# Starting the value projection on unscaled x, and taking the norms' roots on columns of tokens

## The chip, the cores and the metric

The kernel runs on one core of a Trainium2 chip. The metric is the device time of one execution in microseconds. Five engines take part, each with its own in-order queue: TensorE (matmuls, shown as PE, its weight loads as PEld), VectorE (DVE), ScalarE (ACT), GpSimd (POOL) and SyncE (SP), which issues all the transfers.

## What is computed

```python
# x: (1, 2048, 1024) f32; two layers, then one more RMSNorm
h = rms_norm(x, w0)                        # x * rsqrt(mean(x*x) + 1e-6) * w0
u, v, g = split(h @ w_in, 3)               # each 2048 wide
v = layer_norm(gelu(v))                    # over its 2048 columns
s = einsum('gts,bnsgc->bntgc', tril(w_s), v in chunks of 128 tokens) + b_s
x = x + (gelu(u) * s * silu(g)) @ w_out
h = rms_norm(x, w1)
xb, g = split(h @ w_in_b, 2)               # each 1536 wide
xc = causal conv of width 4 over xb        # then two gates of 12 heads of 128
y = linear recurrence over the tokens      # a*h + sqrt(1-a^2)*(i*xc)
x = x + (y * silu(g)) @ w_out_b
return rms_norm(x, wf)
```

## The kernel before

Activations are held transposed, features on the 128 partitions and tokens on the free axis. The 2048 tokens go in two blocks (`i`, NB = 2) of 1024, each in two halves (`th`) of 512. Every f32 factor is split in two rounded parts (`split`, L78: a cast on ScalarE, L80, a difference on VectorE, L81), and a product is three matmuls (`mm3`, L284 to 288).

A block runs through these stages. `a_values` (L570) makes v: for each of four column groups `c` of 512, for each of eight feature tiles `kt`, it multiplies token tiles of 128 (stationary) with the weights (moving, 512 columns), 12 matmuls for a half's four token tiles and one `kt`. The sums stand in PSUM, `pj` (three buffers of two banks) and `pb` (two of one bank). `evict` applies Gelu, takes statistics and stores v to memory. Group 0 goes by halves, the other three take both halves together. Then come `a_gates` (u and g with a Strassen scheme over 2x2 blocks, the spatial gate, `ps`), four `out_round`s, `b_branch` (layer 1: `px`, `pg`, and per head the gates `pr`, `pi`), `b_out` (`po`) and the final norm with `store`.

Weights come from a single ordered list, `stream`. `take(key)` (L270) issues the loads up to 8 entries ahead of the key and the splits up to 4 ahead. In block 0 six of the eight items of layer 0's output weights are prepared and stored away for both blocks (`keep`) during groups 1 to 3, two in each, and the last two in the gate stage.

The norm: `Norm.add` squares on ScalarE and adds on VectorE into `acc` (128 x 512). `finish` (L398) sums over the partitions with one matmul against ones, so the sum of a token stands in all partitions, and calls `rsqrt` (L372) on 128 x 512: Identity and Sqrt on ScalarE, then a reciprocal and three more operations on VectorE for one Newton step. It is used 12 times: for the two halves of each block at layer 0, at layer 1 (`finish_b`) and at the end (`end_f`).

At the start, `first` (half 0 of block 0) is loaded, normed, scaled and split before `a_values` is called; `step(0, 0)` does the same for `second`. `step` also makes Strassen's sums (`Sums`) and sets up the spatial mask and bias (`setup_sgu`) and the recurrence's constants (`setup_lru`). At layer 1, `hb` is x times the norm's weight without 1/rms, and 1/rms is multiplied in when `px` and `pg` are read (`xb` L718, `sg` L739).

The order of the instructions on each engine is fixed when the program is built: a scheduler takes the traced instructions by priority as its estimate of times says that they are ready and have a buffer.

Of the kernel before, what the change touches and what calls it, by code (L numbers as in the profile page):

```python
# [14 lines left out]
P = 128  # L15
D = 1024
# [30 lines left out]

AG = ((0, 0), (1, 0), (0, 1), (1, 1))


@with_exitstack
def trunk(ctx: ExitStack, tc: tile.TileContext, xT, WI, WV, WB, WO, WG, par, wsT, bs, outT):
# [14 lines left out]
    def pb(name):  # L67
        return pbp.tile([P, T], F32, tag="pb", name=name)

    def wk(name):  # L70
        return work.tile([P, 1032], F32, tag="wk", name=name)[:, :TB].rearrange(
            "p (a t) -> p a t", a=2
        )

# [12 lines left out]
    def wop(name):  # L87
        return wops.tile([P, 2, T], F32R, tag="wop", name=name)

    def prep_v(i, c):  # L90
        st = {}

        def load(k):
            def f():
                st[k] = raws.tile([P, 2, T], F32, tag="raw", name=f"rv{i}_{c}_{k}")
                nc.sync.dma_start(
                    st[k], WV[c * 8 + 2 * k : c * 8 + 2 * k + 2].rearrange("k p t -> p k t")
                )
            return f

        def make(kt):
            def f():
                t = wop(f"wv{i}_{c}_{kt}")
                split(t, st[kt // 2][:, kt % 2, :])
                return t
            return f

        return [((i, "v", c, kt), make(kt), load(kt // 2) if kt % 2 == 0 else None)
                for kt in range(8)]

    def prep_item(i, m, keep=False, use=True):

# [150 lines left out]
    def advance(c, n, f):  # L263
        while c[0] < len(stream) and c[1] <= n:
# [2 lines left out]
            c[0] += 1  # L267
            c[1] += key is not None

    def take(key):  # L270
        def load(key, make, load):
            if load is not None:
                load()

        def make(key, make, load):
            t = make()
            if key is not None:
                ready[key] = t

        advance(loads, at[key] + FAR, load)  # L280
        advance(makes, at[key] + LOOK, make)
        return ready.pop(key)

    def mm3(out, sh, sl, mh, ml, first, last):  # L284
# [10 lines left out]
    def col(c):  # L295
        return pp[:, c : c + 1]

    ones = const.tile([P, P], F32, name="ones")
    eps = const.tile([P, 2], F32, name="eps")
    halo = const.tile([P, NH, 3], F32, name="halo")  # L300
    state = const.tile([P, NH], F32, name="state")
    c8 = const.tile([P, NH], F32, name="c8")
# [78 lines left out]
    class Norm:  # L381
# [5 lines left out]
        def add(self, t, eng=nc.vector):  # L387
            for kk in range(2):
# [178 lines left out]
        nc.sync.dma_start(yd[a].rearrange("h p k t -> p h k t")[:, :, j % 2, :], t)  # L567


    def a_values(i, bt, step):  # L570
# [4 lines left out]
        def mm(c, kt, w, tt, out):  # L575
            n, a = kt // 2, kt % 2
            b = bt[a, tt // 4][n // 2]
            ts = slice((tt % 4) * P, (tt % 4 + 1) * P)
            mm3(
                out, b[:, 0, n % 2, ts], b[:, 1, n % 2, ts], w[:, 0], w[:, 1], kt == 0, kt == 7  # L580
            )

        def evict(c, tt, srcs):
            t = wk(f"v{i}_{c}_{tt}")
            if len(srcs) == 1:
                nc.scalar.activation(t, srcs[0], AF.Gelu_apprx_tanh)
            else:
                for k in range(2):
                    nc.scalar.activation(t[:, k], srcs[k], AF.Gelu_apprx_tanh)
# [4 lines left out]
        w = [take((i, "v", 0, kt)) for kt in range(8)]  # L594
        for th in range(2):
            acc = [pj(f"pv{i}_0_{th}{k}") for k in range(2)]
            for kt in range(8):
                for tt in range(4):
                    mm(0, kt, w[kt], 4 * th + tt, acc[tt // 2][:, tt % 2])
                step(0, 8 * th + kt)  # L600
            for k in range(2):
                evict(0, 4 * th + 2 * k, [acc[k]])
        for c in range(1, 4):
            acc = [pj(f"pv{i}_{c}_{k}") for k in range(3)]
            last = [pb(f"pv{i}_{c}_{k}") for k in range(3, 5)]
            for kt in range(8):
                wt = take((i, "v", c, kt))
                for tt in range(8):
                    out = acc[tt // 2][:, tt % 2] if tt < 6 else last[tt - 6]
                    mm(c, kt, wt, tt, out)  # L610
                step(c, kt)
            for k in range(3):
                evict(c, 2 * k, [acc[k]])
            evict(c, 6, last)
# [89 lines left out]
    class Head:  # L704
# [9 lines left out]
        def conv(self, px, rb):  # L714

            n = self.n
            xb = work.tile([P, 1032], F32, tag="wk", name=f"xb{self.id}")
# [207 lines left out]
    bt = {}  # L925
    first.split(bt)
    second = Half(0, 1)
    pending = []
    for i in range(NB):
        tpa = {}  # L930

        def step(c, kt):
            if c > 0:
                return
            if kt == 0:
                if i == 0:
                    second.load(True)
                    second.norm()
                    second.scale()
                second.split(bt)  # L940
            if kt in (1, 3) and pending:
                pending.pop(0)()
            if kt in (8, 12):
                g = (kt - 8) // 4
                have = {1: bt[0, 0][g], 2: bt[1, 0][g], 3: bt[1, 1][g]}
                hx = first.x | second.x
                q = {(a, th): hx[a, th, g] for a in range(2) for th in range(2)}
                tpa[g] = Sums(f"ha{i}_{g}", q, have)
                tpa[g].make(*((5, 6, 7, 4) if g == 0 else (5,)))
            if kt == 14:  # L950
                if i == 0:
                    setup_sgu()
                    setup_lru()
                else:
                    load_sgu(i)

        values = a_values(i, bt, step)
        tpa[1].make(6, 7, 4)
        yd = a_gates(i, [tpa[0].o, tpa[1].o], values)

# [174 lines left out]
```

## Time and profile before

| | us |
|---|---|
| median of 3 runs (2287.63 to 2290.79) | 2289.09 |
| the profiled execution | 2292.71 |
| its span, first to last instruction | 2291.0 |
| TensorE busy | 2213.1 (97%) |
| VectorE busy | 1575.7 (69%) |
| ScalarE busy | 1057.3 (46%) |

Busy time is the union of an engine's instructions; a waiting engine is not busy. The idle time in front of an instruction is what its engine did nothing in, and the name behind it tells what ended that. The columns PEclk give TensorE's granted clock, where 1.00 is 2.4 GHz and 0.50 is 1.2 GHz. On the profile's chain of waits TensorE has 85%, VectorE 8%, transfers 3%.

### The profile page before, as it was taken

Reading aid. Unit: us, or ns where it says so; the run is one execution under the profiler, and the core shown is the slowest. Engines: PE = TensorE matmul, PEld = TensorE weight load, DVE = VectorE, ACT = ScalarE, POOL = GpSimd, SP = SyncE. Lnnn points to the kernel's source line nnn. Section 1 sums busy time; section 2 is a strip of 40 time slices with the busy share of each in tenths; the row PEclk is TensorE's granted clock in tenths of the full one; section 3 lists DMA queues with packets and bytes.
Section 4 is the critical chain, followed back from the end, with each engine's and each line's share of the span. In section 5 each row is a group of like instructions: output and inputs, shape, how many; then the busy total and the mean of one; then the engine's idle time right before and its main releaser. Section 6 shows DMA issues by size and latency. Waiting matters only on the chain.

```text
span 2291.0 us, 25466 instructions
## 1 busy us (share of the span) xinstructions
PE 2213.1 (97%) x9872; PEld 1821.4 (80%) x9872; DVE 1575.7 (69%) x1936; ACT 1057.3 (46%) x1377; POOL 63.2 (3%) x82
## 2 busy tenths in 40 slices
PE   5999999999999899999999999999999989999996
PEld 4787888888788688888788888888878868888884
DVE  6957787676777677775693266676669766776736
ACT  4434444443215677774342144444412347767611
POOL 0000000000000001000000000000000000110000
PEclk9999999999999999999999999999999989999998
DMA  4788353327764122226143233322487512321411
GB/s 148 262 310 307 127 180 111 110 83 270 276 231 141 51 88 88 95 102 231 37 166 110 74 110 111 102 94 100 162 311 256 194 60 69 106 92 65 176 45 74
DMA packets 124040, 327.84 MB, mean 143 GB/s; under 512 B 9616, under 2 KB 26128, under 8 KB 123920
## 3 DMA queue, kind: packets, MB, share of 16 engines
q1 hardware_dynamic: 123920, 326.22, 41.0%
q8 instruction: 77, 1.26, 0.2%
q14 instruction: 43, 0.35, 0.0%
HBM read 232.34 MB, written 93.85 MB: 142 GB/s over the span
## 4 chain that ended last, share of the span: by engine, by line
PE 85%; DVE 8%; DMA 3%; issue 2%; ACT 1%; SPq 0%; DVEq 0%; ACTq 0%
PE J L286 20%; PE pv L286 13%; PE pg L286 11%; PE px L286 10%; PE po L286 10%; PE X L286 6%; PE Y L286 5%; PE Z L286 3%; PE ps L653 2%; PE pr L286 2%; PE pi L286 2%; DMA keep<-wc 1%; DVE ya L81 1%; DMA x<-in_xT 1%; DVE xr L873 0%
## 5 line engine op out<-in xcount | busy, mean ns | idle before, releaser
L286 PE MATMUL pv<-wv,b 128*128 128x512 f32 x1536 | 357.9, 395 | 19.6 <-ACT b L80 15.8
L286 PE MATMUL J<-ha,w 128*128 128x512 f32 x1536 | 368.9, 391 | 0.5 <-DVE u_2b L494 0.5
L286 PEld LDWEIGHTS pv<-wv,b 128*128 128x128 f32 x1536 | 291.4, 190 | 86.4 <-ACT b L80 17.8
L286 PEld LDWEIGHTS J<-ha,w 128*128 128x128 f32 x1536 | 287.6, 188 | 61.5 <-DVE u_2b L494 0.9
L286 PE MATMUL po<-yb,wo 128*128 128x512 f32 x1152 | 265.6, 392 | 2.6 <-DVE xr L862 2.6
L286 PE MATMUL pg<-hb,wb 128*128 128x512 f32 x1152 | 266.6, 390 | 0.0
L286 PE MATMUL px<-hb,wb 128*128 128x512 f32 x1152 | 266.6, 390 | 0.0
L286 PEld LDWEIGHTS po<-yb,wo 128*128 128x128 f32 x1152 | 217.3, 189 | 49.7 <-DVE xr L862 3.0
L286 PEld LDWEIGHTS pg<-hb,wb 128*128 128x128 f32 x1152 | 217.1, 188 | 46.0
L286 PEld LDWEIGHTS px<-hb,wb 128*128 128x128 f32 x1152 | 216.3, 188 | 45.8 <-PE st_b L400 0.5
L286 PE MATMUL J<-b,w 128*128 128x512 f32 x768 | 186.8, 391 | 0.3 <-DVE w L81 0.3
L286 PE MATMUL X<-ya,w 128*128 128x512 f32 x768 | 184.1, 390 | 2.3 <-ACT ya L80 1.3
L286 PEld LDWEIGHTS X<-ya,w 128*128 128x128 f32 x768 | 143.6, 188 | 34.0 <-DVE x L550 2.2
L286 PEld LDWEIGHTS J<-b,w 128*128 128x128 f32 x768 | 142.9, 188 | 30.0 <-DVE w L81 0.7
L80 ACT CAST w<-raw 128x512 fp32r<-128x512 f32 x160 | 99.3, 622 | 139.7 <-issue 66.9
L81 DVE TENSOR_TENSOR w<-raw,w 128x512 fp32r<-128x512 f32 x160 | 109.7, 688 | 61.6 <-ACT w L80 61.2
L80 ACT CAST ya<-ya 128x1024 fp32r<-128x1024 f32 x56 | 57.0, 1049 | 170.7 <-DVE ya L449 92.7
L80 ACT CAST wb<-rb 128x512 fp32r<-128x512 f32 x96 | 58.8, 616 | 99.9 <-PE px L286 49.2
L550 DVE TENSOR_TENSOR x<-x,X 128x1024 f32<-128x1024 f32 x64 | 78.0, 1218 | 35.2 <-PE X L286 35.1
L286 PE MATMUL Z<-ya,w 128*128 128x512 f32 x384 | 94.3, 391 | 3.1 <-DVE ya L81 2.7
L729 DVE SCALAR_TENSOR_TENSOR xc<-xb,pp,xc 128x1024 f32<-128x1024 f32 x72 | 92.3, 1282 | 4.3 <-ACT xc L725 3.5
L286 PE MATMUL Y<-b,w 128*128 128x512 f32 x384 | 93.5, 392 | 0.8 <-DVE sp L657 0.6
(344 smaller groups left out, 2868.0 us busy)
## 6 DMA issues: line engine op xcount, KB each, us to landing
w<-keep SPq DMA_DIRECT2D x112, 512.0 KB, 3.8
raw<-in_w SPq DMA_DIRECT2D x64, 512.0 KB, 3.5
keep<-wc SPq DMA_DIRECT2D x56, 512.0 KB, 5.7
rb<-in_wb SPq DMA_DIRECT2D x48, 512.0 KB, 3.4
rv<-in_v SPq DMA_DIRECT2D x32, 512.0 KB, 4.3
vd<-v SPq DMA_DIRECT2D x32, 512.0 KB, 4.4
vl<-vd SPq DMA_DIRECT2D x32, 512.0 KB, 4.7
ya<-ya SPq DMA_DIRECT2D x16, 1024.0 KB, 5.8
```

The source lines that it names most:

```text
L80: nc.scalar.copy(dst[:, 0], src)
L81: nc.vector.tensor_tensor(dst[:, 1], src, dst[:, 0].bitcast(F32), ALU.subtract)
L286: nc.tensor.matmul(out, lhsT=s, rhs=m, start=first and n == 0, stop=last and n == 2, skip_group_check=True,)
L550: nc.vector.tensor_tensor(t, t, acc[z], ALU.add)
L653: nc.tensor.matmul(pS[:, n * P : (n + 1) * P], lhsT=v[j][th][:, n, cc * P : (cc + 1) * P], rhs=wcv[:, j, :], start=True, stop=True,)
L729: nc.vector.scalar_tensor_tensor(xf, xb[:, k : k + TB], col(C_CW + 4 * n + k), xf, ALU.mult, ALU.add)
```

## The change

The first two groups of block 0 (columns 0 and 1, half 0) multiply `hv`, which is x times the norm's weight, split tile by tile as it lands. 1/rms is put in at the eviction: a token is a partition there, so it is the per-partition scale of the Gelu. Columns 0 and 1 of half 1 follow as groups of their own, with the scaled half, and load and split their weights a second time. Columns 2 and 3 take both halves as before. `Norm.finish` is cut in two: `columns` sums each 128 tokens into one column (tokens on partitions) and takes the root there on 128 x 4, `row` spreads it again over all partitions by a diagonal matrix and a matmul with ones. All 12 norms use them. Two of the prepared items of output weights move into the gate stage, and the set-up steps move to later groups.

```diff
+KT = (0, 2, 1, 3, 4, 6, 5, 7)
+VG = (
+    ((0, ((0,),)), (1, ((0,),)), (0, ((1,),)), (1, ((1,),)), (2, ((0, 1),)), (3, ((0, 1),))),
+    ((0, ((0,), (1,))), (1, ((0, 1),)), (2, ((0, 1),)), (3, ((0, 1),))),
+)
...
-        for c in range(4):
-            units = prep_v(i, c)
-            if i == 0 and c > 0:
+        for k, (c, _) in enumerate(VG[i]):
+            units = prep_v(i, k, c)
+            if i == 0 and k > 3:
                 more = ahead.pop(0) + ahead.pop(0)
...
-            for k in (0, 4):
+            for k in (0, 3, 6, 9):
                 n = ahead.pop(0)
...
+    nc.gpsimd.affine_select(
+        out=ident, in_=ones, pattern=[[1, P]], compare_op=ALU.is_equal, fill=0.0, base=0,
+        channel_multiplier=-1,
+    )
...
+        def columns(self):
+            st = pb(f"st_{self.name}")
+            for n in range(4):
+                nc.tensor.matmul(
+                    st[:, n : n + 1], lhsT=self.acc[:, n * P : (n + 1) * P], rhs=ones[:, 0:1],
+                    start=True, stop=True,
+                )
+            c = self.c = self.acc[:, 0:12].rearrange("p (k n) -> p k n", k=3)
+            rsqrt(c[:, 0], st[:, 0:4], c[:, 1], c[:, 2], 1.0 / D, 0)
+            return c[:, 0]
+
+        def row(self, r):
+            d = sm(f"nd_{self.name}")
+            b = pb(f"bc_{self.name}")
+            for n in range(4):
+                ns = slice(n * P, (n + 1) * P)
+                nc.vector.tensor_scalar(d[:, ns], ident, self.c[:, 0, n : n + 1], None, ALU.mult)
+                nc.tensor.matmul(b[:, ns], lhsT=ones, rhs=d[:, ns], start=True, stop=True)
+            nc.scalar.copy(r, b)
+
         def finish(self, r):
-            st = pb(f"st_{self.name}")
-            nc.tensor.matmul(st, lhsT=ones, rhs=self.acc, start=True, stop=True)
-            rsqrt(r, st, sm(f"nm_{self.name}"), self.acc, 1.0 / D, 0)
+            self.columns()
+            self.row(r)
...
+                    src = srcs[k] if len(srcs) > 1 else srcs[0][:, k]
+                    nc.scalar.activation(
+                        t[:, k], src, AF.Gelu_apprx_tanh,
+                        scale=1.0 if rs is None else rs[:, tt + k : tt + k + 1],
+                    )
...
+        for k, (c, turns) in enumerate(VG[i]):
+            w, n = {}, 0
+            raw = hv is not None and k < 2
+            for ths in turns:
+                tts = [4 * th + t for th in ths for t in range(4)]
+                acc = [pj(f"pv{i}_{k}_{n}{q}") for q in range(min(len(tts) // 2, 3))]
+                last = [pb(f"pv{i}_{k}_{n}{q}") for q in range(len(tts) - 2 * len(acc))]
+                for kt in KT:
+                    if kt not in w:
+                        w[kt] = take((i, "v", k, kt))
...
+                rs = r() if raw else None
+                for q in range(len(acc)):
+                    evict(c, tts[2 * q], [acc[q]], rs)
...
-    first = Half(0, 0)
-    first.load()
-    first.norm()
-    first.scale()
-    first.split(bt)
+    nm0 = Norm("a0_0")
+    for n, (a, g) in enumerate(AG):
+        t = first.x[a, 0, g] = wk(f"xa0_{a}0{g}")
+        o = top(f"hv{a}{g}")
+        hv.setdefault((a, 0), []).append(o)
+        src = xv[g, a][:, :, span(0, 0)]
+        for kk in range(2):
+            if n == 0:
+                nc.sync.dma_start(t[:, kk], src[:, kk])
+                if kk == 0:
+                    advance_to(0)
+            elif kk == 0:
+                nc.sync.dma_start(t, src)
+            w = col(C_NA + 4 * g + 2 * kk + a)
+            nc.scalar.activation(o[:, 0, kk], t[:, kk], AF.Copy, scale=w)
+            nc.vector.scalar_tensor_tensor(
+                o[:, 1, kk], t[:, kk], w, o[:, 0, kk].bitcast(F32), ALU.mult, ALU.subtract
+            )
+            if n == 0:
+                make_to(kk)
+        advance_to(2 * n + 2)
+        make_to(2 * n + 1)
...
+            if k == 0 and n % 2 == 1:
+                a, g = AG[n // 2]
+                nm0.add(first.x[a, 0, g])
+            if (k, n) == (0, 4):
+                second.load(True)
+            if (k, n) == (0, 7):
+                nm0.columns()
+            if (k, n) == (1, 0):
+                second.norm()
+            if (k, n) == (1, 1):
+                second.scale()
                 second.split(bt)
+            if (k, n) == (1, 7):
+                first.r = sm("ra0_0", "rb")
+                nm0.row(first.r)
+            if (k, n) == (2, 0):
+                first.scale()
+                first.split(bt)
+            if (k, n) == (2, 4):
+                setup_lru()
+            if (k, n) == (3, 0):
+                sums(0, 5, 6, 7, 4)
+            if (k, n) == (3, 4):
+                setup_sgu()
+            if (k, n) == (4, 0):
+                sums(1, 5)
```

## Rows read from the trace of the kernel before

**Rows 1.** The page: busy us, share of span, instructions, by engine.

```profile
PE 2213.1 (97%) x9872; PEld 1821.4 (80%) x9872; DVE 1575.7 (69%) x1936; ACT 1057.3 (46%) x1377; POOL 63.2 (3%) x82
```

**Rows 2.** Timeline of TensorE, start: start us, us, instruction, [idle before].

```profile
28.15 2.08 PE L286 MATMUL pv<-wv,b 128*128 128x512 f32 x4 [13.22 <-ACT b L80]
32.19 15.01 PE L286 MATMUL pv<-wv,b 128*128 128x512 f32 x53 [1.96 <-DVE b L81]
47.04 1.02 PE L400 MATMUL st_a<-sa_a,ones 128*128 128x512 f32 x2
...
59.51 1.20 PE L286 MATMUL pv<-wv,b 128*128 128x512 f32 x4 [2.57 <-ACT b L80]
61.70 3.68 PE L286 MATMUL pv<-wv,b 128*128 128x512 f32 x8 [0.99 <-DVE b L81]
```

**Rows 3.** Windows of TensorE: stretch, length, busy (matmuls), granted clock, transfers.

```profile
32.20:37.90 5.70, 5.70 (x13) 1.00 0.00 0
37.90:46.90 9.00, 9.00 (x41) 1.00 0.01 2
61.80:65.20 3.40, 3.40 (x9) 0.51 0.51 195
...
755.20:761.00 5.80, 5.68 (x13) 0.50 0.00 0
...
1871.10:1877.70 6.60, 6.53 (x15) 0.50 0.00 0
```

**Rows 4.** Timeline of ScalarE at the start.

```profile
6.13 0.63 ACT L391 ACTIVATE sa_a<-xa 128x512 f32<-128x512 f32 x1 [4.05 <-DMA xa<-in_xT]
...
7.46 1.21 ACT L394 ACTIVATE sq_a<-xa 128x512 f32<-128x512 f32 x2 [0.18 <-DMA xa<-in_xT]
...
11.78 2.73 ACT L80 CAST wv<-rv 128x512 fp32r<-128x512 f32 x5
```

**Rows 5.** Groups by form, 0 to 60 us: name xcount | busy, mean ns | idle.

```profile
L395 DVE TENSOR_TENSOR sa_a<-sa_a,sq_a 128x512 f32<-128x512 f32 x14 | 9.7, 692 | 12.1 <-ACT sq_a L394 11.5
...
L910 DVE SCALAR_TENSOR_TENSOR xt<-xt,pp,ra 128x512 f32<-128x512 f32 x8 | 5.4, 746 | 0.0
...
L81 DVE TENSOR_TENSOR wv<-rv,wv 128x512 fp32r<-128x512 f32 x8 | 5.1, 679 | 0.4 <-ACT wv L80 0.4
...
L81 DVE TENSOR_TENSOR b<-xa,b 128x1024 fp32r<-128x1024 f32 x4 | 4.6, 1222 | 0.0
...
L375 ACT ACT_TABLE_LOAD x1 | 1.3, 1283 | 0.0
```

**Rows 6.** Groups by form, 222 to 227 us: small operations.

```profile
L640 DVE TENSOR_SCALAR vl<-vl,mv,rstd 128x256 f32<-128x256 f32 x3 | 1.1, 408 | 0.4 <-DMA vl<-vd 0.4
...
L374 ACT ACTIVATE rstd<-mv,eps 128x8 f32<-128x8 f32 x1 | 0.3, 301 | 0.9 <-DVE mv L617 0.9
...
L376 DVE RECIPROCAL rstd<-rstd 128x8 f32<-128x8 f32 x1 | 0.2, 195 | 0.0
```

**Rows 7.** Chain of waits, 0 to 300 us: start us, us, what.

```profile
254.50 1.78 PE ps L653 x16
```

**Rows 8.** Timeline at the entry of layer 1, block 0.

```profile
733.26 1.88 PE L400 MATMUL st_b<-sa_b,ones 128*128 128x512 f32 x4
...
736.99 6.57 DVE L376 RECIPROCAL rbb<-rbb 128x512 f32<-128x512 f32 x2 [2.18 <-ACT rbb L375]
...
747.62 1.22 DVE L718 TENSOR_TENSOR xb<-px,rbb 128x1024 f32<-128x1024 f32 x1
...
755.28 0.80 PE L286 MATMUL pr<-xch,wg 128*128 128x512 f32 x1 [9.21 <-ACT xch L734]
```

**Rows 9.** Timeline of TensorE at the passage to block 1.

```profile
1139.52 5.75 PE L286 MATMUL po<-yb,wo 128*128 128x512 f32 x17 [2.60 <-DVE xr L862]
```

**Rows 10.** Timeline at the end.

```profile
2273.05 1.50 PE L400 MATMUL st_f<-sa_f,ones 128*128 128x512 f32 x2 [4.66 <-DVE sa_f L395]
...
2281.60 5.39 DVE L873 SCALAR_TENSOR_TENSOR xr<-xr,pp,rf 128x512 f32<-128x512 f32 x8
```

More of the change, by code (lines that the diff above doesn't have):

```diff
@@ L70, in wk @@
     def wk(name):
-        return work.tile([P, 1032], F32, tag="wk", name=name)[:, :TB].rearrange(
+        return work.tile([P, 1028], F32, tag="wk", name=name)[:, :TB].rearrange(
             "p (a t) -> p a t", a=2
@@ L88, in wop, with prep_v, load, make @@
         return wops.tile([P, 2, T], F32R, tag="wop", name=name)
-    def prep_v(i, c):
+    def prep_v(i, k, c):
         st = {}
-        def load(k):
+        def load(j):
             def f():
[L95 to L98, printed above, removed]
+                st[j] = raws.tile([P, 2, T], F32, tag="raw", name=f"rv{i}_{k}_{j}")
+                kt = 8 * c + KT[2 * j]
+                nc.sync.dma_start(st[j], WV[kt : kt + 3 : 2].rearrange("k p t -> p k t"))
             return f
-        def make(kt):
+        def make(n):
             def f():
-                t = wop(f"wv{i}_{c}_{kt}")
-                split(t, st[kt // 2][:, kt % 2, :])
-                return t
-            return f
-        return [((i, "v", c, kt), make(kt), load(kt // 2) if kt % 2 == 0 else None)
-                for kt in range(8)]
+                t = wop(f"wv{i}_{k}_{n}")
+                split(t, st[n // 2][:, n % 2, :])
+                return t
+            return f
+        return [((i, "v", k, KT[n]), make(n), load(n // 2) if n % 2 == 0 else None)
+                for n in range(8)]
     def prep_item(i, m, keep=False, use=True):
@@ L268, in advance, with load_one, make_one, advance_to @@
             c[1] += key is not None
-    def take(key):
[L271 to L281, printed above, removed]
+    def load_one(key, make, load):
+        if load is not None:
+            load()
+    def make_one(key, make, load):
+        t = make()
+        if key is not None:
+            ready[key] = t
+    def advance_to(k):
+        advance(loads, k, load_one)
+    def make_to(k):
+        advance(makes, k, make_one)
+    def take(key):
+        advance_to(at[key] + FAR)
+        make_to(at[key] + LOOK)
         return ready.pop(key)
@@ L299, in trunk @@
     eps = const.tile([P, 2], F32, name="eps")
+    ident = const.tile([P, P], F32, name="ident")
     halo = const.tile([P, NH, 3], F32, name="halo")
@@ L588, in evict @@
                 for k in range(2):
-                    nc.scalar.activation(t[:, k], srcs[k], AF.Gelu_apprx_tanh)
+                    src = srcs[k] if len(srcs) > 1 else srcs[0][:, k]
[3 more added lines that the diff above has]
+                    )
             for k in range(2):
@@ L592, in evict @@
             nc.sync.dma_start(vd[c][tt : tt + 2].rearrange("k p t -> p k t"), t)
[L594 to L614, printed above, removed]
+        for k, (c, turns) in enumerate(VG[i]):
[8 more added lines that the diff above has]
+                        w[kt] = take((i, "v", k, kt))
+                    for q, tt in enumerate(tts):
+                        out = acc[q // 2][:, q % 2] if q < 2 * len(acc) else last[q - 2 * len(acc)]
+                        mm(hv if raw else bt, kt, w[kt], tt, out)
+                    step(k, n)
+                    n += 1
+                rs = r() if raw else None
+                for q in range(len(acc)):
+                    evict(c, tts[2 * q], [acc[q]], rs)
+                if last:
+                    evict(c, tts[-2], last, rs)
         mv = const.tile([P, 8, 2], F32, tag="mv", name=f"mv{i}")
@@ L716, in conv @@
             n = self.n
-            xb = work.tile([P, 1032], F32, tag="wk", name=f"xb{self.id}")
+            xb = work.tile([P, 1028], F32, tag="wk", name=f"xb{self.id}")
             nc.vector.tensor_tensor(
@@ L919, in split @@
                     )
-    first = Half(0, 0)
-    first.load()
-    first.norm()
-    first.scale()
-    bt = {}
-    first.split(bt)
-    second = Half(0, 1)
+    first, second = Half(0, 0), Half(0, 1)
+    bt, hv = {}, {}
+    nm0 = Norm("a0_0")
[20 more added lines that the diff above has]
+        make_to(2 * n + 1)
     pending = []
@@ L930, in trunk @@
         tpa = {}
-        def step(c, kt):
-            if c > 0:
-                return
[L935 to L939, printed above, removed]
-                second.split(bt)
[L941 to L955, printed above, removed]
@@ L957, in trunk, with sums, step @@
-        values = a_values(i, bt, step)
+        def sums(g, *ps):
+            have = {1: bt[0, 0][g], 2: bt[1, 0][g], 3: bt[1, 1][g]}
+            hx = first.x | second.x
+            q = {(a, th): hx[a, th, g] for a in range(2) for th in range(2)}
+            tpa[g] = Sums(f"ha{i}_{g}", q, have)
+            tpa[g].make(*ps)
+        def step(k, n):
+            if i > 0:
+                if (k, n) == (0, 0):
+                    second.split(bt)
+                if (k, n) in ((0, 1), (0, 3)):
+                    pending.pop(0)()
+                if (k, n) == (0, 8):
+                    sums(0, 5, 6, 7, 4)
+                if (k, n) == (0, 12):
+                    sums(1, 5)
+                if (k, n) == (0, 14):
+                    load_sgu(i)
+                return
+            if k == 0 and n % 2 == 1:
[9 more added lines that the diff above has]
+                second.scale()
+                second.split(bt)
+            if (k, n) == (1, 7):
[7 more added lines that the diff above has]
+            if (k, n) == (3, 0):
+                sums(0, 5, 6, 7, 4)
+            if (k, n) == (3, 4):
+                setup_sgu()
+            if (k, n) == (4, 0):
+                sums(1, 5)
@@ L958, in trunk @@
+        values = a_values(
+            i, bt, step, hv if i == 0 else None, lambda: nm0.c[:, 0],
+        )
         tpa[1].make(6, 7, 4)
@@ L1123 @@
     arrays = {k: np.ascontiguousarray(a) for k, a in arrays.items()}
-    nc = bacc.Bacc("TRN2", target_bir_lowering=False, num_devices=1, dynamic_dma_scratch_size=1024)
+    nc = bacc.Bacc("TRN2", target_bir_lowering=False, num_devices=1, dynamic_dma_scratch_size=512)
     args = [
```

13 lines of the change are left out of this document (7 added, 6 removed).

## The prediction

> **What bounds the kernel now.** I read the page's first part first: TensorE is busy for 97% of the span [rows 1], so only two things can move the time, the matmul passes themselves and the places where TensorE stands still or runs at its lower clock. The timeline of TensorE shows where it stands; span less busy time is 2291.0 - 2213.1 = 77.9 us, some 16 of them behind its last matmul, and a few places hold most of the rest. At the start it computes nothing of v before 28.15 us, stops again until 32.19, and around 60 us waits twice for the second half of the tokens [rows 2]. At the entry of each layer-1 pass (two of them, at 755 and 1871 us) it stands 9.21 us before the first gate matmul `pr` [rows 8]. At the passage to the second block of tokens it stands 2.60 us [rows 9], and after its last projection the final norm's chain runs alone [rows 10].
>
> The windows give the clock's share. In 37.9 to 46.9 us, 40 whole matmuls take 9.0 us, 0.225 us each: that is 2.4 GHz. In 32.2 to 37.9 there are 13 in 5.7 us, 0.44 each, the lower level of 1.2 GHz (the granted column still says 1.00 here, the pace tells it); 61.8 to 65.2 (granted 0.51), 755.2 to 761.0 (0.50) and 1871.1 to 1877.7 (0.50) are stretches like it, each behind one of the idle times [rows 3]. What such a stretch costs is its length less 0.225 us for each matmul in it.
>
> **The change part by part.**
>
> *The start (A).* Before, the first matmul of v waited for the whole norm: x loaded, squared, summed, rooted on 128x512, scaled, split. Now it waits for half an x tile, one pair of weight tiles and a split of each. ScalarE begins on the first x tile at 6.13 us and on the next at 7.46, so 512 KB land each 1.33 us [rows 4]. Half a tile in front then lands near 6.13 - 0.66 = 5.5, the weights behind it at 6.8, the cast takes 0.6 (five in 2.73 us, [rows 4]) and the difference on VectorE 0.68 [rows 5]: 8.1 us. Ends: 6.8 (landed, nothing else) and 13.1, if the weights came as late as before, when their first cast began at 11.78 [rows 4]. I take 8.1, the pace of the nearest rows: 28.15 - 8.1 = 20.0 us gained. Once started it is fed: eight steps need 8 x 512 KB, all there by some 15 us, and each step costs VectorE two differences and an add (about 2.0 us), against 2.7 us of TensorE for 12 matmuls.
>
> The idle 1.96, 2.57 and 0.99 us [rows 2] go, 5.5. In their place comes the new wait. The first two groups' Gelu waits for a column of 1/rms: after the last matmul of group 0, eight column passes (0.9, below), Identity 0.30, a table load 1.28 for Sqrt, Sqrt (no more than Identity), a reciprocal of 0.20 and three operations no longer, a table load for Gelu beside them, and two Gelus of some 0.6: about 5.2 us [rows 5, 6]. Group 1 has one free pair of PSUM banks; its second pair waits for that eviction, and on the in-order TensorE everything of group 1 behind it. Six matmuls (1.4 us) surely go first; if the issue order takes the later steps of the free pair first, up to 24 do (5.4 us). So 0 to 3.8 us idle; I take 1.7. Behind the waiting Gelu on ScalarE stand the weight casts of groups 1 and 2 and the second half's squares, for which group 2 waits: VectorE has some 44 us of work (three groups' weights 24 x 0.68, hv 8 x 0.68, two norms' adds 14 x 0.69, scale 5.4, split 4.6 [rows 5], statistics and small things) for 46 us before group 2. But group 2 needs the parts of the second half one after the other, so I take 1.5 us here, with 0 and 10 as ends. Idle time saved: 5.5 - 3.2 = 2.3.
>
> Half clock before: 4 matmuls in 2.08 us [rows 2] lost 1.2, 13 in 5.7 lost 2.8, 9 in 3.4 lost 1.4 [rows 3], 5.4 in all. After, one stretch like the 5.7 us one remains, 2.8: 2.6 saved. TensorE's own work grows: see (E); two norms now lie in this stream instead of one, 2 x 1.78 - 0.87 = 2.7 lost. A = 20.0 + 2.3 + 2.6 - 2.7 = 22.2 us.
>
> The Trainium skill speaks against this part: "ScalarE: Activation LUTs", Table sets, counts about 2.7 us for each switch of set, where the row has 1.28 [rows 5]. By it the first eviction would come 2.8 us later and the sum would be that much smaller; the trace does not agree with that figure, and I stay with the row.
>
> Weights of columns 0 and 1 are now loaded and split twice: 8 more loads of 512 KB on SyncE's queue, 16 more casts and differences. They lie beside 87 us of matmuls in which nothing of layer 0's output weights is prepared any more; two of those items move into the gate stage (two loads, seven stores, about 7.6 us of VectorE each), beside 84 matmuls, 19 us, per pair of steps. Cost 0; if VectorE had no room there, up to 5 us. The mask and bias set-up and the LRU constants move from the first group to the third and fourth, at the same cost. The second half's four loads move four steps back on SyncE's queue, behind the first weights; it is wanted 40 us later. The identity on GpSimd and the memsets behind it have no reader for 30 us. Narrower work tiles and a smaller scratch change no instruction.
>
> *What a root on columns costs (E).* Before: one sum matmul of two passes over 512 columns, 1.88 us for two norms with their tail [rows 8], 0.87 each in place. After: four weight loads times two passes with one column each, and four 128-column matmuls of two passes. The row for 128x128 in f32 is 1.78 us for 16 passes, 0.111 each [rows 7]. The one-column passes load the same weights, so I take 0.111 for them too (from below: nothing). That is 16 x 0.111 = 1.78, 0.91 more per norm (ends 0.0 and 0.9). Of 12 norms, two are in A, four in B, one is the last; the other five lie in full stretches: E = -4.6.
>
> "TensorE: Matmul & The Clock Gate", Back-to-back issue gap, of the Trainium skill gives a floor of about 25 ns between starts, however few the columns. By it the eight column passes would take 0.2 us, an estimate, in place of 0.9, and E would be near -1; no row here shows a matmul of one column.
>
> VectorE's part falls from 5.4 us (a reciprocal of 3.3, half of 6.57 [rows 8], and three passes of 0.69, as the adds of that size in [rows 5]) to four times 0.20 at most, plus four multiplications with the identity, some 0.25 each (between the 0.20 of 128x8 and the 0.41 of 128x256, [rows 6]): 1.8. ScalarE: Identity, Sqrt and a copy of 0.6 like the casts, less than the two passes over 512 columns before.
>
> *Layer 1's entry (B).* The two reciprocals take 736.99 to 743.56, and three passes for each half follow; `xb` starts at 747.62, `pr` at 755.28, 7.66 later [rows 8]. Now: the first half's sums at about 734.2, Identity 0.3, table load 1.28, Sqrt 0.2, VectorE 0.8, four multiplications 1.0, their matmuls 0.5, copy 0.6: 739; the second half queues behind the first on each engine, 740.5. Then `xb` about 7 us earlier and `pr` at 748.2. TensorE is through with `px` at 746.07 now, and at 747.9 with the 1.8 us of new passes of two norms, so nearly nothing is left of the wait: 1.2 us with the wait for `xcl`. What is late next is `px` itself. Per pass: 9.21 idle and (13 in 5.8 us, 15 in 6.6) 2.9 and 3.2 of half clock go, 1.8 + 1.2 come. B = 12.1 + 12.4 - 6.0 = 18.5; ends 6 (only the reciprocals' length counts, half of it lost in queues) and 24.5.
>
> *The passage to block 2 (C).* `po` waits 2.60 us for VectorE, whose queue in front holds two norms' roots; 2 x 3.6 us of those go. Idle 2.60 and some 1.4 of half clock as in [rows 3] go: C = 4.0, ends 0 and 4.0.
>
> *The end (D).* From the last sum at 2273.05 to the scaling at 2281.60 are 8.55 us [rows 10]. Now, at half clock: column passes 1.8, Identity and Sqrt 0.55, VectorE 0.8 and 1.0, last matmul 0.7, copy 0.6: 5.45. The first half's root leaves VectorE earlier, so one of the last adds is done before the last `xr`: 1.3. D = 4.4, ends 2 and 5.5.
>
> Sum: 22.2 + 18.5 + 4.0 + 4.4 - 4.6 = 44.5 us. The profiled execution took 2292.7 us, 3.6 over the median, so 2248.2 for one like it and 2244.6 for the median.
>
> **The rivals.**
>
> R1, *VectorE is the bound at the start*: group 2 stands 10 us for its half and 1.4 at half clock. For it: 44 us of work in 46. Against it: now the whole chain of the second half costs only 3.6 us of idle time [rows 2]. Sum 44.5 - 9.9: 2254.5 us.
>
> R2, *the roots are shorter, the chain isn't*: it has two more hops (VectorE to TensorE, TensorE to ScalarE), each behind other work in an in-order queue, bursts of matmuls and casts. At 4 us per layer entry, B = 10 and C = 2: 2255 us.
>
> R3, *slower*: each norm now stops at two places of TensorE's queue, at its columns and at its row matmuls. If the row matmuls stand right behind the columns, TensorE waits for Identity, Sqrt and VectorE (1.7 us) and for whatever block VectorE holds in front, the eight scalings of 5.39 us [rows 10] being the longest: 7.1 us in each of ten norms. It decides from 4.5 us per norm on; at 7.1 it costs 71 and the kernel takes 2316 us. Against it: now the sum for the second half stands between other matmuls at 47.04 without idle time in front [rows 2], so the issue order does place such passes where their inputs are ready.
>
> R4, *the start isn't what it says*: the weights land no earlier than now, 13.1 us: 2249.6.
>
> **How the numbers follow.** Forecast 0.60 (R4 in it), its own range 2234 to 2251; R1 0.13; R2 0.14; R1 and R2 together (2265) 0.05; R3 0.05, rest 0.03. The range 2233 to 2264 leaves out R3 and most of the double case, and with it the lower ends of A and B at once. A measurement tells 0.2%, 4.6 us, from no change: faster 0.92, same 0.02, slower 0.06.
>
> **What would show it.** A: first `pv` near 8 us and no idle time over 4 us up to 200. B: `pr` within 2 us of the last `px`, no half clock there. C: no idle time in front of `po`. E: 16 short passes per norm in under 2 us. It is wrong if group 2 stands for VectorE, if `xb` starts more than 3 us later than told, or if TensorE idles in front of row matmuls.

## The result, and the profile after

The changed kernel takes 2254.6 us (2252.49 to 2256.53, 4 runs), the kernel before in the same runs 2288.36 (2287.39 to 2290.79): a ratio of 0.9851, 95% interval 0.9834 to 0.9868. It is 33.8 us shorter. The forecast was 44.5 us, 2244.6. The measured time lies in the range, but outside the likeliest case's own 2234 to 2251.

The profiled execution took 2253.91 us, its span 2252.2. The spans differ by 38.8 us, the medians by 33.8: the profiled execution of before lay 4.4 us over the median of these runs, that of after 0.7 below. What follows accounts for the 38.8.

Idle time in front of TensorE's instructions adds up to 61.2 us before and 25.0 after. TensorE's busy time, by the page against [rows 1], is 4.1 us longer than 2213.1: the new passes, less the half-clock time that went. The time behind TensorE's last matmul fell from 16.4 to 10.0 us.

The start, TensorE's timeline (start, length, instruction, count, in brackets the idle time in front and what ended it), against [rows 2]:

```profile
7.99 24.59 PE L299 MATMUL pv<-wv,hv 128*128 128x512 f32 x96 [2.29 <-ACT wv L87]
32.42 0.95 PE L420 MATMUL st_a<-ones,sa_a 128*128 128x1 f32 x8
33.23 1.65 PE L299 MATMUL pv<-wv,hv 128*128 128x512 f32 x6
...
37.54 1.13 PE L435 MATMUL bc_a<-nd_a,ones 128*128 128x128 f32 x8 [0.18 <-DVE nd_a L434]
38.43 6.85 PE L299 MATMUL pv<-wv,hv 128*128 128x512 f32 x29
```

The first matmul of v stands at 7.99, and from there to 190 us nothing waits for longer than 0.3 us. The eight column passes take 0.81 us of TensorE (32.42 to 33.23), the eight row passes 0.89. Behind the sums TensorE goes on with the free pair of banks of group 1. ScalarE meanwhile, same columns:

```profile
33.46 0.26 ACT L392 ACTIVATE sa_a<-st_a,eps 128x4 f32<-128x4 f32 x1 [0.78 <-PE st_a L420]
...
34.25 1.28 ACT L393 ACT_TABLE_LOAD   x1
...
36.21 1.28 ACT L631 ACT_TABLE_LOAD   x1
37.51 2.42 ACT L631 ACTIVATE v<-pv,sa_a 128x512 f32<-128x512 f32 x4
```

From the last sum to the Gelu are 37.51 - 33.23 = 4.3 us, two table loads of 1.28 in it. Nobody waits for them.

The windows of TensorE (stretch, length, busy time and matmuls, granted clock), against [rows 3]:

```profile
60.00:190.00 130.00, 130.00 (x571) 1.00 0.76 275
201.00:207.90 6.90, 5.30 (x13) 0.51 1.06 403
723.00:738.00 15.00, 11.85 (x44) 0.89 0.07 29
1831.00:1846.00 15.00, 12.15 (x48) 0.89 0.05 20
```

The second line was not foreseen: in the gate stage of block 0 there is now a stretch at 1.2 GHz, behind a wait that was not there before. The last two hold the entries of layer 1, which keep half-clock time.

The first of these entries, all engines, against [rows 8] (some rows of it):

```profile
711.17 1.08 PEld L420 LDWEIGHTS st_b<-ones,sa_b 128*128 128x128 f32 x8
711.40 0.95 PE L420 MATMUL st_b<-ones,sa_b 128*128 128x1 f32 x8
...
715.76 1.05 PE L435 MATMUL bc_b<-nd_b,ones 128*128 128x128 f32 x8
...
716.65 0.95 PE L420 MATMUL st_b<-ones,sa_b 128*128 128x1 f32 x8
716.85 0.58 ACT L436 COPY rbb<-bc_b 128x512 f32<-128x512 f32 x1 [2.68 <-PE bc_b L435]
...
720.73 0.59 ACT L436 COPY rbb<-bc_b 128x512 f32<-128x512 f32 x1 [0.27 <-PE bc_b L435]
...
721.35 1.22 DVE L762 TENSOR_TENSOR xb<-px,rbb 128x1024 f32<-128x1024 f32 x1 [0.17 <-ACT rbb L436]
...
729.02 0.50 PE L299 MATMUL pr<-xch,wg 128*128 128x512 f32 x1 [2.85 <-ACT xch L778]
```

The wait in front of `pr` fell from 9.21 to 2.85 us in both passes. From the first sums to `xb` there are 9.95 us. The second half's sums stand at 716.65, behind the first half's row matmuls.

The passage to block 1's tokens, against [rows 9]: the last `po` and the first `pv`, with no idle time in front of either:

```profile
1124.83 3.11 PE L299 MATMUL po<-yb,wo 128*128 128x512 f32 x13
1127.78 2.43 PE L299 MATMUL pv<-wv,b 128*128 128x512 f32 x10
```

The end, against [rows 10]: from the last sum to the scaling 6.37 us in place of 8.55, all of TensorE's part at half clock:

```profile
2236.47 1.86 PE L420 MATMUL st_f<-ones,sa_f 128*128 128x1 f32 x8 [3.56 <-DVE sa_f L413]
...
2239.71 0.87 DVE L434 TENSOR_SCALAR nd_f<-ident,sa_f 128x128 f32<-128x128 f32 x4
...
2240.14 2.04 PE L435 MATMUL bc_f<-nd_f,ones 128*128 128x128 f32 x8 [1.81 <-DVE nd_f L434]
2242.22 0.58 ACT L436 COPY rf<-bc_f 128x512 f32<-128x512 f32 x1 [3.35 <-PE bc_f L435]
2242.84 3.40 DVE L917 SCALAR_TENSOR_TENSOR xr<-xr,pp,rf 128x512 f32<-128x512 f32 x5 [2.26 <-ACT rf L436]
```

The stage lengths, by the first matmul of each stage in the two traces (worked out from the timelines, us):

| stage | before | after | |
|---|---|---|---|
| up to the first `pv` | 28.15 | 7.99 | -20.16 |
| v, block 0 | 189.90 | 182.78 | -7.12 |
| gates, block 0 | 330.95 | 336.68 | +5.73 |
| layer 1 up to `po`, two blocks | 618.41 | 606.67 | -11.74 |
| `po`, block 0 | 139.70 | 137.15 | -2.55 |
| v, block 1 | 176.12 | 177.80 | +1.68 |
| `po` and end, block 1 | 157.03 | 154.70 | -2.33 |
| the rest | 650.72 | 648.43 | -2.29 |

### The profile page after: what moved, and what is told of

It is laid out like the page before. It is cut to its first block, busy times and chain, and to the rows that moved or that the text cites. A ratio compares the mean times of both kernels' runs of the same rounds, so it can differ in the third digit from the quotient of the medians.

```text
span 2252.2 us, 25966 instructions
## 1 busy us (share of the span) xinstructions
PE 2217.2 (98%) x10040; PEld 1837.2 (82%) x10040; DVE 1544.7 (69%) x2008; ACT 1069.1 (47%) x1417; POOL 60.5 (3%) x83
## 4 chain that ended last, share of the span: by engine, by line
PE 93%; DVE 3%; DMA 2%; ACT 1%; issue 0%; DVEq 0%; SPq 0%; ACTq 0%
PE J L299 22%; PE pv L299 14%; PE po L299 12%; PE pg L299 12%; PE px L299 11%; PE X L299 7%; PE Y L299 6%; PE Z L299 4%; PE ps L697 2%; PE pr L299 2%; PE pi L299 2%; DMA raw<-in_w 1%; DVE ya L88 1%; DMA keep<-wc 0%; DVE xc L773 0%
## 5 line engine op out<-in xcount | busy, mean ns | idle before, releaser
L299 PE MATMUL pv<-wv,b 128*128 128x512 f32 x1344 | 306.7, 390 | 0.0
L299 PEld LDWEIGHTS pv<-wv,b 128*128 128x128 f32 x1344 | 252.0, 188 | 52.9 <-issue 0.5
L88 DVE TENSOR_TENSOR wv<-rv,wv 128x512 fp32r<-128x512 f32 x80 | 53.5, 686 | 71.3 <-ACT wv L87 71.2
L87 ACT CAST wv<-rv 128x512 fp32r<-128x512 f32 x80 | 49.0, 619 | 112.3 <-PE pv L299 98.2
```

Source lines behind the costliest of these rows:

```text
L87: nc.scalar.copy(dst[:, 0], src)
L88: nc.vector.tensor_tensor(dst[:, 1], src, dst[:, 0].bitcast(F32), ALU.subtract)
L299: nc.tensor.matmul(out, lhsT=s, rhs=m, start=first and n == 0, stop=last and n == 2, skip_group_check=True,)
```

## The experiments

The experiments ran in two sets, each on one chip beside the kernel before, which took 2289.19 us in the first set (e1 to e4) and 2289.41 in the second (e5 to e8).

**e1, the start alone.** The old sum matmul and root on 128x512 for all norms but the very first.

```diff
 def finish(self, r):
-    self.columns()
-    self.row(r)
+    st = pb(f"st_{self.name}")
+    nc.tensor.matmul(st, lhsT=ones, rhs=self.acc, start=True, stop=True)
+    rsqrt(r, st, sm(f"nm_{self.name}"), self.acc, 1.0 / D, 0)
```

> The change's start is kept; in all norms but that of the first half, finish goes back to one sum matmul and a root on 128x512. Theory: the parts stand for themselves. The two entries of layer 1 (11.7 us between the two profiles), the passage to block 2 and the end (about 5 us together) are lost again: 2271 us. Rival, VectorE is the bound at the start: the second half's root holds VectorE 3.6 us longer while group 2 waits for that half, TensorE stands there, and the time is 2276 us or more.

Measured 2269.49 us (2267.03 to 2272.39), ratio 0.9915 [0.990, 0.9929]. The entry of layer 1 has its old wait, TensorE's timeline:

```profile
733.54 0.80 PE L299 MATMUL pr<-xch,wg 128*128 128x512 f32 x1 [9.21 <-ACT xch L779]
```

The time is 1.5 us under the 2271 of the theory. The start ends where it does in the changed kernel, to 0.3 us (the first `pv` at 7.51, the v stage 182.99), so the start's gain needs columns in no norm but the first. Of the rival, TensorE standing for VectorE at the start, there is one wait of 1.07 us, at 72.01. The gate stage is just as long as in the changed kernel, 337.09: its loss comes with the start's part of the change, which also reorders the stream of weights.

**e2, the columns alone.** The kernel before with `columns` and `row` in `finish`; nothing of the start moved (the work tiles and the scratch are as small as in the changed kernel).

> The kernel before with nothing but the roots on columns in its 12 norms. Theory: the first matmul of v still waits for the whole norm, but its root is 6 us shorter (first v near 22 us instead of 28), the wait for the second half near 60 us goes (3.6 us idle and 1.5 us of half clock), and the entries of layer 1 and the rest give 16 us: 2288 - 27 = 2261 us. Then most of what the two parts give at the start is one and the same. Rival, the parts add up: the columns give only what the start alone leaves, 2288 - 16 = 2272 us.

Measured 2267.3 us (2266.76 to 2267.98), ratio 0.9905 [0.9889, 0.9922], between the two. TensorE at the start:

```profile
19.59 2.05 PE L422 MATMUL bc_a<-nd_a,ones 128*128 128x128 f32 x8 [5.00 <-DVE nd_a L421]
24.84 2.08 PE L286 MATMUL pv<-wv,b 128*128 128x512 f32 x4 [3.20 <-ACT b L80]
```

Here the predicted second stop of a norm is seen: 5.00 us in front of the row matmuls, for VectorE's `nd`. The first `pv` came 3.3 us earlier and the v stage was 5.8 shorter than before. The new start cuts into the same two stretches, so these 9.1 us can be had only once: the gains of e1 and e2, 19.7 and 21.9, add to 41.6, where both parts together gave 33.8 (37.8 when the changed kernel was run again, e8). Layer 1's waits were 2.87 and 2.86, as in the changed kernel: B, C and D belong to the columns. The gate stage took 331.74, no loss.

**e3, all column sums first.** In `finish_b`, layer 1's norm:

```diff
-                nm[th].finish(rb[:, th])
+                nm[th].columns()
+            for th in range(2):
+                nm[th].row(rb[:, th])
```

> The changed kernel, but at the entry of layer 1 both halves' columns are traced before both rows. Theory: the second half's sums stood behind the first half's row matmuls only because that row held the second of two PSUM buffers; now both sums run at once, 1/rms is complete 3.3 us earlier, pr follows px with no idle time and no half clock: 2.85 us and some 1.5 us less in each pass, 2254.6 - 8.5 = 2246 us. Rival: the queues of ScalarE and VectorE set that time, not the buffer; pr stays 2.85 us behind px and the time 2254.6 us.

Measured 2248.0 us (2243.97 to 2249.38), ratio 0.9817 [0.9803, 0.9832]. All engines, some rows:

```profile
707.20 1.84 PE L420 MATMUL st_b<-ones,sa_b 128*128 128x1 f32 x16
...
712.45 1.95 PE L435 MATMUL bc_b<-nd_b,ones 128*128 128x128 f32 x16
...
715.05 1.23 DVE L762 TENSOR_TENSOR xb<-px,rbb 128x1024 f32<-128x1024 f32 x1 [1.70 <-ACT rbb L436]
...
723.55 0.50 PE L299 MATMUL pr<-xch,wg 128*128 128x512 f32 x1 [1.65 <-ACT xch L778]
```

From the first sum to `xb` 7.85 us in place of 9.95, and 1.65 in front of `pr` in place of 2.85. The layer-1 stages are 1.2 and 2.0 us shorter than in the changed kernel; the rest of the 6.6 us lies elsewhere, 3.4 of it in the gate stage of block 0, which kept its full clock in the profiled execution. So the queue in front of the second half is real, but it is worth 3.2 us here and not the 8.5 that were expected: 1.65 us of the wait stay in each pass, and in the first pass the half clock still follows. That the time comes near the expected 2246 is in part luck.

**e4, the copy ahead of the casts.** The gate stage's wait ends with ScalarE's copy of `u_0a`, in front of which two casts wait for a late load (SyncE's issue, VectorE, ScalarE and TensorE of the changed kernel, some rows):

```profile
195.87 0.35 SPq L126 DMA_DIRECT2D raw<-in_w  x1
...
200.14 0.69 DVE L135 TENSOR_TENSOR s<-raw 128x512 f32<-128x512 f32 x1 [2.08 <-DMA raw<-in_w]
...
200.92 0.62 ACT L87 CAST w<-s 128x512 fp32r<-128x512 f32 x1 [3.70 <-DVE s L135]
...
201.44 0.61 ACT L87 CAST w<-raw 128x512 fp32r<-128x512 f32 x1
...
201.96 0.58 ACT L516 COPY u_0a<-J 128x512 f32<-128x512 f32 x1
...
202.59 6.61 PE L299 MATMUL J<-ha,w 128*128 128x512 f32 x17 [3.48 <-ACT u_0a L516]
```

The load is issued at 195.87 and the difference `s` starts on it at 200.14; the first cast needs `s`, the copy stands behind the casts on ScalarE, and `J` behind the copy. The same place in the kernel before, where the first matmul of the stage starts at 218.05 (190.77 in the changed kernel), SyncE and ScalarE:

```profile
223.79 0.35 SPq L119 DMA_DIRECT2D raw<-in_w  x1
224.44 0.57 ACT L477 COPY u_0a<-J 128x512 f32<-128x512 f32 x1
...
228.89 0.62 ACT L80 CAST w<-s 128x512 fp32r<-128x512 f32 x1 [3.88 <-DVE s L128]
...
232.74 0.59 ACT L484 COPY u_0a<-J 128x512 f32<-128x512 f32 x1 [2.70 <-PE J L286]
233.44 0.62 ACT L80 CAST w<-s 128x512 fp32r<-128x512 f32 x1
```

There the load was as late: issued 5.74 us behind the stage's first matmul, where it is now 5.10, and the cast 10.84 behind it, now 10.15. But both copies stood ahead of the casts. The edit puts the first copy there again.

```diff
-            nc.scalar.copy(self.oa[:, 0], self.J[:, 0])
+            self.first = nc.scalar.copy(self.oa[:, 0], self.J[:, 0]).ins
...
+            if self.id == "0_0":
+                with tc.issue_after(self.first):
+                    self.mm(2, y, True)
```

> The changed kernel; ScalarE's one copy of the first product u of block 0 is queued ahead of the cast w<-s that it stood behind. Theory: TensorE's new stand of 3.48 us in the gate stage came from that order, since the cast waits for a weight load that lands at 200.1 us; with the copy ahead no stand over 1 us is left between 190 and 215 us and no half clock: 2254.6 - 6 = 2248.6 us. Rival: the late load itself holds TensorE, because the next product needs that weight; the stand only moves, and the time stays within 1 us of 2254.6.

Measured 2252.92 us (2251.29 to 2256.37), ratio 0.9844 [0.9829, 0.9859]: no gain that can be told. The wait moved to the next copy of the same tile (ScalarE, then TensorE):

```profile
205.73 0.62 ACT L87 CAST w<-s 128x512 fp32r<-128x512 f32 x1 [6.24 <-DVE s L138]
206.25 0.58 ACT L523 COPY u_0a<-J 128x512 f32<-128x512 f32 x1
...
206.89 4.61 PE L299 MATMUL J<-ha,w 128*128 128x512 f32 x12 [3.20 <-ACT u_0a L523]
```

The gate stage is as long as without this edit, 336.61. So moving one copy is not enough, and the stand only moves, as the rival had it. It does not refute the order as the cause: the second copy now stands behind the second cast (205.73), where it stood ahead of it in the kernel before (232.74 against 233.44), and the edit does not restore that. Nor is the rival's reason shown: the difference for that second cast ran at 204.95, behind scalings of `vl` for whose load VectorE had waited 1.58 us. A version with both copies ahead was not run.

**e5, the items later.** The four prepared items stand one pair later (pair k is entry k, counted from 0, of the stage's list of 16 weight items), so that pair 1's second load has none of their loads and stores ahead of it; ScalarE still has the first cast ahead of the first copy. In the kernel before, the items stood at the pairs 0 and 4, so there too one stood ahead of this load.

```diff
-            for k in (0, 3, 6, 9):
+            for k in (1, 4, 7, 10):
```

> The changed kernel, with the four prepared items of output weights in the gate stage at the pairs 1, 4, 7 and 10 in place of 0, 3, 6 and 9. The two casts of `w` still stand ahead of the copy of `u_0a` on ScalarE, but the load of pair 1's second half has no item's loads ahead of it any more. Theory (the late load is the cause: the cast waits for a difference that waits for a load issued at 195.87 and landed at 200.11 in the changed kernel): the wait of 3.48 us before the first use of `J` near 202.6 us and the 6.9 us at half clock around it go, the gate stage takes 331 us as before the change instead of 336.7, and the time falls by 5 to 6 us, to 2249. Rival (the place of the casts ahead of the copy is enough by itself): a wait of 2 us or more stays at the copy of `u_0a`, the gate stage stays above 334 us, and the time stays within 2 us of 2254.6.

Measured 2248.25 us (2246.62 to 2250.12), ratio 0.982 [0.9806, 0.9833]. ScalarE:

```profile
189.01 0.63 ACT L87 CAST w<-s 128x512 fp32r<-128x512 f32 x1
...
193.69 0.57 ACT L516 COPY u_0a<-J 128x512 f32<-128x512 f32 x1
```

The cast of `w` from `s` still stands ahead of the copy, but runs at 189.01 and holds up nothing. The 20 us from 195 to 215 have no idle time and no half clock. The stage takes 332.64, 1.7 more than before the change (one wait of 1.11 us at 218.81 remains). So the order costs nothing when the load is early, as the late load cost nothing in the old order: the wait needs both. The 3.4 us under the changed kernel beside it (e8) are not all the edit's. Of 4.8 us between the two spans the gate stage gives 1.65 (against the first execution of the changed kernel 4.0). The v stage gives 1.60, where this execution had the full clock from 6.21 us on, and the second pass of layer 1 gives 1.65, where this time no half clock followed the same wait of 2.85 us.

**e6, both.** The edits of e3 and e5 together.

> Both at once: all column sums of layer 1's norm ahead of the row matmuls, and the items at the pairs 1, 4, 7 and 10. If the two losses are independent, the gains add: 2248.0 less 5 to 6 us, 2242.5. Rival (one of them is only covered by the other, or the wait in the gate stage is found again elsewhere): 2247 to 2249, no better than with the sums first alone.

Measured 2243.36 us (2242.25 to 2244.74), ratio 0.9798 [0.9785, 0.9812], the fastest version. The two gains add: it is 8.3 us under the changed kernel beside it (e8), where e3 and e5 stand 3.6 and 3.4 under that, e3 from the other set. TensorE's windows:

```profile
195.00:215.00 20.00, 20.00 (x91) 1.00 0.64 234
715.00:730.00 15.00, 13.05 (x57) 1.00 0.10 35
1821.00:1836.00 15.00, 13.05 (x56) 1.00 0.13 35
```

None of these stretches is at half clock any more; the layer-1 stages take 300.9 us each, 2.5 less than the mean of after.

**e7, the first tile of x whole.**

```diff
-            if n == 0:
-                nc.sync.dma_start(t[:, kk], src[:, kk])
-                if kk == 0:
-                    advance_to(0)
-            elif kk == 0:
+            if kk == 0:
                 nc.sync.dma_start(t, src)
+                if n == 0:
+                    advance_to(0)
```

> The changed kernel, with the very first tile of x loaded whole (512 KB) in place of two halves, the first weights behind it. Theory (the start is bound by what must land: half a tile at 5.3, weights at 6.6, first product at 8.0): 256 KB more ahead of the weights, at the 240 to 400 GB/s that the transfers reach there, 0.6 to 1.1 us, puts the first matmul at 8.6 to 9.1 us, and the time goes up by as much, to 2255.5. Rival (later tiles set the pace of the first pass anyway): the first matmul is later by as much but TensorE waits less behind it, and the time stays within 0.3 us of the changed kernel on the same chip; that can be told from the end of the first pass in the traces.

Measured 2257.54 us (2255.3 to 2258.72), ratio 0.9859 [0.9845, 0.9872]: 5.9 us slower than the changed kernel beside it. Both theories missed. The first `pv` is only 0.29 us later (8.12 against 7.83). Windows of TensorE, this kernel, then the changed one beside it:

```profile
7.50:20.00 12.50, 11.88 (x39) 0.73 1.05 406
...
90.00:120.00 30.00, 27.80 (x117) 1.00 0.80 302
```

```profile
7.50:20.00 12.50, 12.02 (x45) 0.86 1.03 384
...
90.00:120.00 30.00, 30.00 (x129) 1.00 0.85 298
```

By 20 us it is 6 matmuls behind (1.35 us at 2.4 GHz): the granted clock was full from 4.05 us here, low from 7.47 to 14.29; there it was full from 5.53 and low from 8.94 to 12.35. That this is the edit's doing is not shown: the warm-up matmuls start at 1.06 us in every kernel, and with one and the same start code e3 to e6 and e8 had the full clock for the first time at 4.37 to 6.40 us and, in the same 12.5 us, 45 to 53 matmuls. Another 2.2 us are waits between 90 and 120 us, where 16 small set-up operations (4.22 us) stand in front of the weights on VectorE. In the changed kernel the same 16 cost TensorE nothing. The gate stage took 336.83. Its wait there is 3.57 us, as in the first execution of the changed kernel (3.48) and not as beside it (2.44). Why stays open, and with it how much of the 5.9 us is the edit's.

**e8, the changed kernel again,** beside e5 to e7.

> The changed kernel itself once more, on the same chip as the three others, so that differences of 2 us between them are not those of two chips: 2254.6, within 1.5 us, and in the trace the wait of 3.5 us near 202.6 and the two of 2.85 us at `pr`.

Measured 2251.62 us (2250.14 to 2253.97), ratio 0.9837 [0.9824, 0.9851]: 3 us under the first measurement, where 1.5 was expected at most. The two waits at `pr` came as expected (2.86 and 2.85). The wait in the gate stage was shorter in the profiled execution and no half clock followed it; the stage took 334.29:

```profile
200.88 5.51 PE L299 MATMUL J<-ha,w 128*128 128x512 f32 x23 [2.44 <-ACT u_0a L516]
```

So one kernel has a wait at this place with and without a fall of the clock. With the wait 1.0 us longer and the fall behind it the stage took 2.4 us more.

## Why the prediction was right, and where it was not

**A, the start: right in kind, too small.** 20.0 us was forecast to the first `pv` and 20.16 came, in part by luck. The half tile and the weights landed as told (5.34 and 6.62 us, told 5.5 and 6.8). But ScalarE, which was counted as free to cast at once, first loaded a table (1.28 us, at 5.41) and scaled x, and cast only at 7.33; and the first product needed the cast alone, not the difference that was counted (8.13 to 8.81). Behind it 2.2 was forecast and 7.12 came. The two terms that failed are the new idle times, 1.7 us for the first eviction and 1.5 for group 2: neither came (0.2 us in all). The first eviction took about 1 us more than its price (from the last matmul of group 0, 32.42, to the end of two Gelus near 38.7 it is 6.3, told 5.2), but the issue order puts group 1's matmuls on its free pair of banks into that time. VectorE kept up in front of group 2, so R1 didn't come, with the 44 us of work in 46 that was counted for it. Also 0.70 us at 175.75 went. The first 15 matmuls took 6.20 us, 6.20 - 15 x 0.225 = 2.8 lost to the lower clock, as forecast for this execution; e4 and e5, with the same start code, had a v stage 2.1 us shorter than the changed kernel's with fewer of its first matmuls at the low clock. R4's late weights did not come: the first cast of `wv` ends before 7.99. Each of the eviction's two table loads took 1.28 us again, and the instruction behind each starts 0.02 us later (35.55 and 37.51). The Trainium skill's "ScalarE: Activation LUTs", Table sets, has about 2.7 for a switch; no row here shows more than the load itself.

**The gate stage was costed at nothing and got 5.7 us longer, for a reason that the prediction did not weigh.** It counted VectorE's room, 7.6 us for each item moved there, and the bytes. The sentence "Cost 0; if VectorE had no room there, up to 5 us" came near the size with its upper end, but named the wrong resource. The wait is 3.48 us, and the half clock that came with it costs 5.30 - 13 x 0.225 = 2.4. The wait takes two things together: a load that lands 9 us into the stage, and ScalarE's casts ahead of the copies. The load was as late in the kernel before, with an item at pair 0 ahead of it there too; the two more items stand behind it in the list, so they did not delay it. What is new is the order on ScalarE: the copies stand ahead of the casts in the kernel before and in e2 (gate stage 331.74), behind them in the changed kernel and in e1 (337.09). e5 shows that the new order is harmless once the load is early; e4 restored the old order for one copy of two only. Which part of the new start turned the order round is not shown.

**B, the entries of layer 1: the size was wrong, 18.5 forecast, 11.7 measured.** The step that failed is "the second half queues behind the first on each engine, 740.5", 1.5 us for the second half. Measured: the second copy of `rbb` 3.88 us behind the first, because the second half's sums stand behind the first half's row matmuls in TensorE's queue (716.65, where the first half's ended at 712.2), and then go through Identity, Sqrt and four VectorE operations by themselves. `xb` came 9.95 us behind the start of the first sums, not 7.3 (733.26 to 740.6 as told); to `pr` it is another 7.67, as before (7.66). So 2.85 us remained where 1.2 was forecast, and the half clock followed that wait in both passes (0.89 granted over the 15 us): 1.4 and 1.3 us, busy time less 0.225 for each matmul, that were told to go. B's own sign, `pr` within 2 us of the last `px` and no half clock, did not come. This is R2's mechanism, priced at B = 10, not the forecast. e3 and e6 show it from the other side: with the sums first and no half clock the two passes are 8.2 and 8.5 us shorter than before, 16.7 in all, and the 1.65 us left are near the 1.2.

**C and E: right.** The idle time in front of `po` went, with its half clock, 4.0; the two new norms in the stage take 1.66 of it back: 2.3, measured 2.55. A norm's passes take 0.81 + 0.89 = 1.70 us where 1.78 was forecast, so 0.83 more than before; block 1's v stage, with two norms in it, is 1.68 us longer, and just as long (177.80) in e2, where nothing but the norms changed. The one-column passes took 0.10 us each, nearly as the 128-column ones (0.11); each has its own weight load, and the eight loads take 1.08 us (PEld, at 711.17). The Trainium skill's "TensorE: Matmul & The Clock Gate", Back-to-back issue gap, has a floor of about 25 ns between starts; by that eight would be 0.2 us, an estimate, and the trace has 0.81. The same section of the Trainium skill says that in a stream of weight loads and matmuls the spacing comes from both, so the floor was the wrong price for passes that each load their own weights.

**D, the end: 8.55 to 6.37, forecast 5.45.** The row matmuls run at half clock, 2.04 us, and start only when half of the products with the identity are there; from the first product to the copy are 2.5 us where 1.7 was told.

**The sum.** By terms: A -27.3 (told -22.2), gates +5.7 (told 0), B -11.7 (-18.5), C with its norms -2.6 (-2.2), v of block 1 +1.7 (+1.8), the end -2.3 (-3.5), the rest -2.3 (0; of this the output stages, nowhere over 1.4 us, were not followed up). That is 38.8 where 44.5 was told, so two errors of 6 and 7 us were partly hidden by a third of 5 us with the other sign; that the time lies within 10 us of the forecast owes something to that. The other 4 us between 2244.6 and 2254.6 are the profiled executions' places in their runs. R3 did not come in the changed kernel: no row matmul but the last norm's has TensorE wait for more than 0.2 us. e2 had one such stop of 5.00 us, at the start, where nothing else is there to run.

## What to carry to other kernels

When a change makes a program's fixed order anew, look for loads that were late before and cost nothing: what stands behind such a load's reader on an in-order engine decides whether the engine that computes now waits for it, and room on the engines says nothing of that. When a root or a reduction is made cheap for two halves, put both halves' first steps ahead of either's last in the in-order queue; a shorter operation that is queued behind the other half's return trip gives part of the gain back (here 1.2 us of wait in each pass). A wait can be paid twice, by itself and by the half clock that comes with it, 1.3 to 2.4 us a time here: price the low-clock matmuls as well, as a chance and not as a certainty.

## What was not expected of the hardware

A matmul of one f32 column costs the same 0.10 us per pass as one of 128 columns (0.95 us busy for 8, against 1.05). And the length of a wait alone did not decide whether the lower clock came with it. In the changed kernel it did at a wait of 3.48 us (0.51 from 201 to 207.9) and at both of 2.85 us; in e5 it did at one wait of 2.85 us and not at the other. In e6 two waits of 1.65 us at `pr` left the clock at its full level, in e3 one of two such waits did not.
